# The lower half of every split weight tile on VectorE alone, in a fused gMLP, sparse-attention and differential-attention kernel

## The chip, the cores and the metric

The kernel runs on one core of one Trainium2 chip. The metric is the device time of one execution in microseconds (us), as the median over the runs shown; each run's time comes with a profile of one execution. The engines are TensorE (PE, with its weight loads as PEld), VectorE (DVE), ScalarE (ACT), GpSimd (POOL) and the DMA queue of SyncE (SP).

## What is computed

512 tokens of width 1024 pass through three layers, all in fp32:

```
first_block, layer 0:  x += g1 * rms(gmlp(mod(rms(x))));      x += g2 * rms(relu(h @ w1)^2 @ w2)
first_block, layer 1:  x += g1 * rms(nsa(mod(rms(x)), kv));   x += g2 * rms(relu(h @ w1)^2 @ w2)
second_block:          x += gate * (concat(stick_breaking(h), diff_attention(h)) @ w_out)
mod(h) = h * (1 + scale) + shift;  scale, shift, g = split(c_act @ ada_w + ada_b)
gmlp:  u, v = split(gelu(h @ w_in)); out = (u * (causal w_s @ layer_norm(v) + b_s)) @ w_out
nsa:   16 heads on 4 key/value groups; compressed, selected and windowed branches, gated
```

The weights are read once each: 205 MB over the execution by the profile's page.

## The kernel before

**Split products.** TensorE multiplies in fp32r, which holds fewer bits than fp32. So every operand of a large product is held as two tiles, an upper part `hi` (a copy of the source rounded to fp32r) and a lower part `lo = src - hi`, and one product is three matmuls: hi by hi, hi by lo, lo by hi. Three names of tiles recur: `wh`/`wl` are the two parts of a weight tile, `twh`/`twl` those of a weight tile in the tail of an output product, `ah`/`al` and `tah`/`tal` those of an activation that an output product reads. `raw` is the loaded weight before it is split; there are four places for it in the weight path (`RAW = 4`), and four each for `wh` and `wl` (`WT = 4`).

**Who makes the parts.** `splitw` (line 724) makes both from a source in SBUF. The upper part goes through `copyw`, which offers three engines (an ACT copy, a DVE copy, a POOL `tensor_scalar`). The lower part goes through `flex`, which offers two: a `tensor_sub` on DVE or on POOL. `splitw` is called for the weight tiles (`w_fm`, `w_rows`, `out_gemm`), the activations of the output products (`act_f32`), the normed activations (`h_split`, `gmlp`) and the probabilities of the attention stages (`ptl`, `ptc`, `sS`, with their upper parts `pth`, `ptc`, `sS`). Another function, `split` (line 719), for sources in PSUM, is fixed to ACT and DVE.

**What sets the order.** Nothing runs when it is written down: a recorder, `Rec`, keeps every operation with its readers and writers, and `Rec.order` lays all of them out with a list scheduler before the first instruction is issued. The scheduler has a modelled duration for each operation on each engine it may run on, adds 300 ns to an alternative on DVE and 100 ns to one on POOL when it compares alternatives, and knows that a two-input operation on POOL and one on DVE hold each other up. It runs twelve passes (`PASSES`), each with the due dates that the pass before gave, and keeps the pass with the earliest modelled end. So one operation that may no longer go to POOL can change the place of others on every engine, and also the order in which SP issues transfers. PE's order is fixed by hand within the attention stages (`KSEQ`, `NSEQ`, `SEQ`). Since the recorder issues all operations, each has the line L615 in the profile (activation tables L609), and rows are told apart by tile.

**The stages**, in time of the profile: set-up and the first layer's gMLP with its output product up to 190 us; the first feed-forward up to some 560; the key/value side of the sparse attention up to 640; the sparse attention (NSA) up to 880; the second feed-forward up to 1280; the second block's projections, stick-breaking and differential attention up to 1545; its output product to the end. At the start, `setup` builds eight `diag` tiles on DVE, from which PE makes `cb`, a broadcast of the conditioning vector; each weight row of `ada_w` is then multiplied with `cb` on DVE and summed (the operation `raw<-raw,cb`), which gives the vectors scale (`B`), shift (`S`) and gate (`G`). `wide` (line 948) spreads such a vector over all partitions for a stage's end: SP writes it to DRAM, then reads it back as two broadcasts (`S2w<-S` and then `S2w<-S2w`; likewise `B2w`, `G1w`). The gMLP's output product (`out_gemm` with `ATAIL = 8`) has all its eight weight rows as tail tiles, and chunk by chunk of 128 tokens passes through all eight; after each chunk the `boundary` makes the residual and the next layer's input `hx`, with `B2w` and `S2w`, which PE turns round (`tp`).

Of the kernel before, what the change touches and what calls it, by code (L numbers as in the profile page):

```python
# [26 lines left out]
F32 = mybir.dt.float32  # L27
# [643 lines left out]
class KB:  # L671
# [52 lines left out]
    def splitw(self, hi, lo, src):  # L724

        self.copyw(hi, src)
        self.flex("tensor_sub", lo, src, hi.bitcast(F32))

    def copyw(self, dst, src):

# [1345 lines left out]
```

## Time and profile before

| | before |
|---|---|
| median of 3 runs | 1586.44 us (1580.53 to 1587.76) |
| profiled execution: time, span of its instructions | 1586.38 us, 1584.6 us |
| granted clock of TensorE, mean over the span | 0.984 |
| busy share of the span | PE 95%, PEld 79%, DVE 70%, ACT 42%, POOL 27% |
| HBM traffic | 205 MB read, 6 MB written, 134 GB/s over the span |

The span is the time from the first to the last instruction; some 1.8 us of the execution lie around it. A group's mean duration can be read beside the shortest and the median of the same tile: where the mean lies far above, some of these instructions were held up while they ran. Which engine a wait is put down to is inferred from semaphore events.

### The profile page before, as it was taken

How to read it: one execution, taken by the hardware profiler on the slowest of the kernel's cores; microseconds unless marked ns; L12 is line 12 of the kernel's file. 1: busy time of each engine (PE TensorE's matmuls, PEld its weight loads, DVE VectorE, ACT ScalarE, POOL GpSimd, SP SyncE). 2: the span in 40 equal slices, each digit the busy share in tenths (PEclk: the TensorE clock that was granted, in tenths of full speed). 3: DMA queues.
4: the chain of work that ended last, by engine and by line, in shares of the span. 5: the costliest groups of instructions: out<-in, count | busy, mean ns of one | idle time of the engine just before them, and what ended most of it. 6: DMA issues, size and time to landing. Idle time of an engine off the chain costs nothing. (4 is left out here: it accounts for less than half of the span.)

```text
span 1584.6 us, 20197 instructions
## 1 busy us (share of the span) xinstructions
PE 1508.1 (95%) x7410; PEld 1256.2 (79%) x7410; DVE 1103.8 (70%) x1957; ACT 667.5 (42%) x1443; POOL 425.7 (27%) x415
## 2 busy tenths in 40 slices
PE   4997899999999999999998999999999999999988
PEld 3786788888888889787876898888888888878777
DVE  6897686567874478777886684555674568688882
ACT  4441342222121456577786332222111337667680
POOL 4044100000111131475676000000242024243560
PEclk9998899999999999999998999999999999999999
DMA  9756189537841071300115256538512251112312
GB/s 347 238 186 173 30 292 288 187 133 276 340 154 40 28 249 54 112 1 28 28 31 170 67 200 182 172 111 252 180 45 67 89 181 54 54 54 55 80 47 100
DMA packets 151395, 212.98 MB, mean 134 GB/s; under 512 B 49536, under 2 KB 110208, under 8 KB 151296
## 3 DMA queue, kind: packets, MB, share of 16 engines
q1 hardware_dynamic: 151296, 211.69, 41.7%
q8 instruction: 58, 0.95, 0.3%
q14 instruction: 41, 0.34, 0.1%
HBM read 205.33 MB, written 6.34 MB: 134 GB/s over the span
## 5 line engine op out<-in xcount | busy, mean ns | idle before, releaser
L615 DVE TENSOR_TENSOR wl<-raw,wh 128x1024 fp32r<-128x1024 f32 x176 | 230.9, 1315 | 55.7 <-PE fmps L615 18.5
L615 DVE CAST wh<-raw 128x1024 fp32r<-128x1024 f32 x118 | 88.7, 752 | 123.5 <-PE fmps L615 96.7
L615 PE MATMUL acc<-wh,ah 128*128 128x512 f32 x432 | 168.9, 392 | 0.0
L615 PE MATMUL acc<-wl,ah 128*128 128x512 f32 x432 | 168.6, 392 | 0.0
L615 DVE SCALAR_TENSOR_TENSOR raw<-raw,cb 128x1024 f32<-128x1024 f32 x112 | 146.4, 1329 | 6.7 <-DMA raw<-in_kv_ada_w_dram 6.0
L615 PE MATMUL acc<-wh,al 128*128 128x512 f32 x432 | 134.5, 391 | 0.0
L615 ACT ACTIVATE r<-fmps 128x512 f32<-128x512 f32 x64 | 38.4, 599 | 210.7 <-PE fmps L615 210.7
L615 POOL TENSOR_TENSOR al<-hid,ah 128x512 fp32r<-128x512 f32 x10 | 16.9, 1694 | 401.2 <-ACT ah L615 388.8
L615 PE MATMUL acc<-twh,tah 128*128 128x512 f32 x272 | 107.2, 402 | 3.3 <-DVE twh L615 3.3
L615 PE MATMUL acc<-twl,tah 128*128 128x512 f32 x272 | 107.3, 403 | 3.1 <-DVE twl L615 3.1
L615 PE MATMUL fmps<-hfh,wl 128*128 128x512 f32 (+1 forms) x288 | 106.0, 368 | 2.3 <-DVE wl L615 2.3
L615 PE MATMUL fmps<-hfl,wh 128*128 128x512 f32 (+1 forms) x288 | 105.6, 367 | 0.0
L615 PE MATMUL fmps<-hfh,wh 128*128 128x512 f32 (+1 forms) x288 | 105.4, 368 | 0.1
L615 PE MATMUL fmps<-hf1l,wh 128*128 128x512 f32 (+1 forms) x288 | 105.2, 366 | 0.0
L615 PE MATMUL fmps<-hf1h,wl 128*128 128x512 f32 (+1 forms) x288 | 105.2, 366 | 0.0
L615 PE MATMUL fmps<-hf1h,wh 128*128 128x512 f32 (+1 forms) x288 | 104.8, 365 | 0.0
L615 ACT CAST ah<-hid 128x512 fp32r<-128x512 f32 x47 | 29.1, 619 | 157.7 <-PE acc L615 157.7
L615 PEld LDWEIGHTS acc<-wl,ah 128*128 128x128 f32 x432 | 81.6, 189 | 16.9
L615 PEld LDWEIGHTS acc<-wh,ah 128*128 128x128 f32 x432 | 81.4, 189 | 16.8
L615 PEld LDWEIGHTS acc<-wh,al 128*128 128x128 f32 x432 | 81.4, 189 | 16.7
L615 PE MATMUL acc<-twh,tal 128*128 128x512 f32 x272 | 88.2, 400 | 3.2 <-DVE tal L615 3.2
L615 ACT CAST wh<-raw 128x1024 fp32r<-128x1024 f32 x57 | 59.3, 1049 | 55.9 <-PE fmps L615 25.7
(561 smaller groups left out, 3995.0 us busy)
## 6 DMA issues: line engine op xcount, KB each, us to landing
raw<-in_ada_w_dram SPq DMA_DIRECT2D x40, 1024.0 KB, 7.5
raw<-in_ff_w_in_dram SPq DMA_DIRECT2D x32, 1024.0 KB, 10.5
raw<-in_ff_w_out_dram SPq DMA_DIRECT2D x32, 1024.0 KB, 5.0
raw<-in_w_in_dram SPq DMA_DIRECT2D x16, 1024.0 KB, 5.6
raw<-in_w_ada_dram SPq DMA_DIRECT2D x12, 1024.0 KB, 11.1
raw<-in_a_w_in_dram SPq DMA_DIRECT2D x8, 1024.0 KB, 8.6
raw<-in_ada_w_dram SPq DMA_DIRECT2D x16, 512.0 KB, 11.9
raw<-in_kv_ada_w_dram SPq DMA_DIRECT2D x8, 1024.0 KB, 14.2
```

The source lines that it names most:

```text
L615: getattr(real[e], m)(*a, **k)
```

## The change

`splitw` makes the lower part on DVE always. Nothing else is edited; the order of everything is derived anew by the same rule.

```
@@ -724,7 +724,7 @@
     def splitw(self, hi, lo, src):
 
         self.copyw(hi, src)
-        self.flex("tensor_sub", lo, src, hi.bitcast(F32))
+        self.dve.tensor_sub(lo, src, hi.bitcast(F32))
```

In the order lists, 87 subtractions leave POOL: 30 of 128x1024 (`wl` 18, `twl` 12), 45 of 128x512 (`al` 11, `tal` 18, `hbl` 3, `hkl` 1, `vl` 3, `dV` 3, `ptl` 6) and 12 smaller (`sS` 3, `ptc` 8, one of a compression weight). DVE's list has all of them. POOL has 22 more one-input copies and scalings than before, ACT 21 fewer; PE has the same 7408 matmuls and transposes, with local changes of order. Six of the 128x1024 and nine of the smaller subtractions that leave POOL lie in the NSA stage, eleven and seventeen in the second block.

First place: DVE at the start, from the `diag` tiles on (`hx` is the scaled input, `x_87` and `x_94` two chunks of it, `cbp` the PSUM of `cb`). Before:

```order
L615 TENSOR_SCALAR diag<-ident,cc 128x128 x8
L615 SCALAR_TENSOR_TENSOR xrs<-rt,xrs 128x4
L615 TENSOR_SCALAR hx<-x_87,xrs 128x512
L615 COPY cb<-cbp 128x512
L615 SCALAR_TENSOR_TENSOR raw_100,S_186<-raw_100,cb 128x1024
L615 SCALAR_TENSOR_TENSOR raw_100,B_215<-raw_100,cb 128x1024
```

and now:

```order
L615 TENSOR_SCALAR diag<-ident,cc 128x128 x8
L615 SCALAR_TENSOR_TENSOR xrs<-rt,xrs 128x4
L615 TENSOR_SCALAR hx<-x_87,xrs 128x512
L615 TENSOR_SCALAR hx<-x_94,xrs 128x512
L615 TENSOR_TENSOR wl<-raw,wh 128x1024 x2
L615 SCALAR_TENSOR_TENSOR raw_100,B_192<-raw_100,cb 128x1024
L615 SCALAR_TENSOR_TENSOR raw_100,S_207<-raw_100,cb 128x1024
```

The first two `wl` stand on DVE between `diag` and the first dot product; before, they were POOL's, whose list there was `wh`, `wl` twice, `hx`, and is now `wh` and four `hx`. The copy of `cb` that DVE had went to ACT.

Second place: SP ahead of and during the gMLP's output product (the weight of that product is `a_w_out`; `G_546` and `G_520`, `B_834` and `B_876`, `S_1000` and `S_981` are the same vectors before and now). A piece of the difference:

```order
+L615 DMA raw<-in_a_w_out_dram 128x2x1024
+L615 DMA G1w<-G_520 128x8x1
+L615 DMA B2w<-B_876 128x8x1
 L615 DMA raw<-in_a_w_out_dram 128x2x1024
 L615 DMA G1w<-G1w 128x512 x2
-L615 DMA raw<-in_a_w_out_dram 128x2x1024 x3
-L615 DMA S2w<-S_1000 128x8x1
+L615 DMA B2w<-B2w 128x512 x2
+L615 DMA raw<-in_a_w_out_dram 128x2x1024 x2
+L615 DMA S2w<-S_981 128x8x1
 L615 DMA S2w<-S2w 128x512 x2
-L615 DMA B2w<-B_834 128x8x1
-L615 DMA B2w<-B2w 128x512 x2
```

The first `a_w_out` is ahead of the write of `G1w` (before, behind it), `B2w` is written and read back ahead of the last weights, and `S2w` alone is left for the end, where `S2w` and then `B2w` stood.

Third place: DVE through the gMLP's output product (`mx` and `sg` belong to the mixing ahead of it). Before:

```order
L615 CAST twh<-raw 128x1024
L615 SCALAR_TENSOR_TENSOR mx<-pm,lngb,E 128x512 x2
L615 TENSOR_TENSOR twl<-raw,twh 128x1024
L615 SCALAR_TENSOR_TENSOR mx<-pm,lngb,E 128x512
L615 TENSOR_TENSOR sg_722<-sg_722,mx 128x512
L615 TENSOR_TENSOR twl<-raw,twh 128x1024
L615 SCALAR_TENSOR_TENSOR raw,S_1000<-raw,cb 128x1024
L615 TENSOR_TENSOR tal<-sg_722,tah 128x512
L615 SCALAR_TENSOR_TENSOR raw,S_1000<-raw,cb 128x1024
L615 TENSOR_TENSOR twl<-raw,twh 128x1024
L615 TENSOR_TENSOR S_1000<-S_1000,vcol 128x8
```

and now:

```order
L615 TENSOR_TENSOR twl<-raw,twh 128x1024
L615 TENSOR_TENSOR tal<-sg_730,tah 128x512
L615 TENSOR_TENSOR twl<-raw,twh 128x1024
L615 TENSOR_TENSOR tal<-sg_937,tah 128x512
L615 TENSOR_TENSOR twl<-raw,twh 128x1024
L615 SCALAR_TENSOR_TENSOR raw,S_981<-raw,cb 128x1024
L615 TENSOR_TENSOR tal<-sg_937,tah 128x512 x2
L615 TENSOR_TENSOR S_981<-S_981,vcol 128x8
L615 CAST twh<-raw 128x1024
L615 TENSOR_TENSOR twl<-raw,twh 128x1024 x2
```

All eight `twl` and eight `tal` of this product are DVE's (six and four before), its `B` is done ahead of the product, and the sum that ends `S` stands behind six of the eight `twl` where it stood behind three.

## Rows read from the trace of the kernel before

**Rows 1.** Page, part 1: busy time, share of the span, instructions of each engine.

```profile
PE 1508.1 (95%) x7410; PEld 1256.2 (79%) x7410; DVE 1103.8 (70%) x1957; ACT 667.5 (42%) x1443; POOL 425.7 (27%) x415
```

**Rows 2.** Stretches: length; PE, PEld, DVE, ACT, POOL busy us; clock, DMA share, GB/s.

```profile
0.00:45.00 45.00, 21.47 (x83) 15.88 (x84) 28.85 (x52) 21.46 (x35) 17.33 (x14) 0.95 0.94 327
45.00:80.00 35.00, 35.00 (x152) 28.82 (x151) 28.91 (x58) 16.03 (x28) 2.78 (x2) 0.97 0.73 241
...
125.00:190.00 65.00, 50.41 (x239) 41.27 (x238) 46.90 (x63) 18.25 (x36) 26.66 (x14) 0.84 0.41 100
...
800.00:880.00 80.00, 72.19 (x392) 56.90 (x391) 57.95 (x157) 52.76 (x140) 49.69 (x59) 0.94 0.36 100
880.00:1280.00 400.00, 399.80 (x1885) 335.22 (x1883) 241.50 (x344) 102.12 (x198) 44.01 (x24) 1.00 0.45 143
...
1480.00:1545.00 65.00, 58.41 (x314) 49.15 (x313) 55.61 (x109) 47.85 (x126) 43.33 (x30) 0.97 0.14 49
```

**Rows 3.** A group by shape: count, busy us, mean ns; idle time before, and its releasers.

```profile
L615 DVE TENSOR_TENSOR wl<-raw,wh 128x1024 fp32r<-128x1024 f32 x176 | 230.9, 1315 | 55.7 <-PE fmps L615 18.5 <-ACT wh L615 18.5 <-PE acc L615 11.5
```

**Rows 4.** Tiles on DVE: shortest, median and longest duration in ns.

```profile
L615 DVE TENSOR_TENSOR wl<-raw,wh x176: 1194/1225/3415, 46.3 to 1542.9; 128x1024 fp32r<-128x1024 f32 x176
...
L615 DVE TENSOR_TENSOR al<-hid,ah x38: 671/684/1773, 333.6 to 1193.3; 128x512 fp32r<-128x512 f32 x38
...
L615 DVE TENSOR_SCALAR diag<-ident,cc x8: 273/275/2380, 13.0 to 18.6; 128x128 f32<-128x128 f32 x8
```

**Rows 5.** What PE waited for: us in total, times, longest.

```profile
PE tp L615 <- DVE hx L615: 5.2, 2, 5.0
...
PE acc L615 <- DVE tal L615: 3.2, 1, 3.2
PE acc L615 <- DVE twl L615: 3.1, 2, 1.9
```

**Rows 6.** Timeline of the start: start, us, engine, operation [idle before].

```profile
12.99 5.85 DVE L615 TENSOR_SCALAR diag<-ident,cc 128x128 f32<-128x128 f32 x8
13.14 4.64 POOL L615 TENSOR_TENSOR wl<-raw,wh 128x1024 fp32r<-128x1024 f32 x2
...
24.36 3.37 DVE L615 SCALAR_TENSOR_TENSOR raw<-raw,cb 128x1024 f32<-128x1024 f32 x1
...
29.73 1.12 PE L615 MATMUL vps<-wh,hh 128*128 128x512 f32 x2 [2.59 <-ACT hh L615]
```

**Rows 7.** Timeline of the gMLP's output product and boundary, SP and DVE.

```profile
156.70 1.21 DVE L615 SCALAR_TENSOR_TENSOR raw<-raw,cb 128x1024 f32<-128x1024 f32 x1
...
156.80 0.37 SPq L615 DMA_DIRECT2D S2w<-S  x1
167.92 1.23 SPq L615 DMA_DIRECT2D S2w<-S2w  x2
...
178.14 0.80 SPq L615 DMA_DIRECT2D B2w<-B2w  x2
...
182.07 0.69 DVE L615 TENSOR_TENSOR hx<-x,B2w 128x512 f32<-128x512 f32 x1 [5.54 <-DMA B2w<-B2w]
```

**Rows 8.** Timeline of the differential attention.

```profile
1500.64 2.57 POOL L615 TENSOR_TENSOR twl<-raw,twh 128x1024 fp32r<-128x1024 f32 x1
...
1500.88 2.88 DVE L615 SCALAR_TENSOR_TENSOR dPA<-dPA,rr 128x512 f32<-128x512 f32 x1
...
1522.70 0.74 DVE L615 SCALAR_TENSOR_TENSOR dPA<-dPA,rr 128x512 f32<-128x512 f32 x1
```

**Rows 9.** Chain that ended last: start, us, engine, tile.

```profile
1540.91 1.36 POOL al L615
...
1544.89 35.20 PE acc L615 x155
```

**Rows 10.** Timeline of the stick-breaking attention, POOL's copies beside DVE.

```profile
1315.60 1.64 DVE L615 TENSOR_TENSOR wl<-raw,wh 128x1024 fp32r<-128x1024 f32 x1
...
1316.58 0.94 POOL L615 TENSOR_SCALAR ptc<-saC 128x256 fp32r<-128x256 f32 x1 [0.40 <-POOL sbh L615]
```

More of the change, by code (lines that the diff above doesn't have):

```diff
@@ L726, in splitw @@
         self.copyw(hi, src)
-        self.flex("tensor_sub", lo, src, hi.bitcast(F32))
+        self.dve.tensor_sub(lo, src, hi.bitcast(F32))
     def copyw(self, dst, src):
```

## Prediction

> **What bounds the kernel now.** I read the page's busy times first. PE is busy 1508.1 of 1584.6 us and DVE 1103.8 [rows 1], so a faster DVE pays only where PE stands still, 76.5 us in all. The stretches tell where [rows 2]. In the second feed-forward (880 to 1280 us) PE is busy 399.8 of 400 us: whatever DVE does there, nothing is to be had. From 45 to 80 us it is busy 35 of 35. It stands still 23.5 us in the first 45 us, 14.6 us between 125 and 190 (the gMLP's output product), 7.8 us between 800 and 880 (end of NSA) and 6.6 us between 1480 and 1545 (differential attention). Between 125 and 190 the granted clock is also 0.84: since the levels are 1.2 and 2.4 GHz, 32% of that stretch, 20.8 us, ran at the lower one, in which half of the work, 10.4 us, is lost.
>
> The rows of single operations then tell what POOL's subtractions cost. A `wl` on DVE takes 1.225 us in the median, 1.315 in the mean and 3.415 at the longest [rows 3, 4]; 176 times the difference of mean and median is 16 us of being held up on this tile alone. Neighbours show it better. Eight `diag` take 5.85 us while POOL makes two `wl` in 4.64 us [rows 6]; the median `diag` is 0.275 us [rows 4]. One `dPA` takes 2.88 us beside a `twl` on POOL, another 0.74 us [rows 8]. So a subtraction that spares DVE 1.2 us can hold it up by about 2 us, and it takes POOL itself some 2.3 to 2.6 us [rows 6, 8].
>
> **What the change moves.** By the order lists 30 subtractions of 128x1024 and 57 smaller ones go to DVE. At 1.225 us and at most 0.684 us (the `al` [rows 4], of 128x512) that is 36.8 + 39.0 = at most 75.8 us more work on DVE. Against it stands the hold-up that goes away. No single row has its sum, so the bounds are nil and all the time those 87 took on POOL, at some 2.4 us for a wide one and half of that for the others 140 us. I take it to be about as large as the added work, because the rows on neighbours show 3.65 us for two subtractions at the start and 2.1 us for one later, against 1.225 each. DVE's busy time should therefore stay near 1100 us, and what counts is the place. By stage:
>
> *Start, -4 us (0 to -6).* PE's first matmul waits for `diag`. Eight of them undisturbed take 8 x 0.275 = 2.2 us, so 3.65 us go. The dot product at 24.36 us took 3.37 us [rows 6], undisturbed 1.21 [rows 7]: 2.16 us go. The two `wl` (2.45 us) and one more `hx` (at most 0.68) now lie on DVE ahead of the dot products. They fit into the time in which DVE waits for `cb` to come from PE; if they do not, 3.1 us of the 5.8 are given back. I take 4. The start of the `vps` products at 29.73 us [rows 6] moves up by that, and as PE is busy without a gap from 45 us on, the gain is kept if the loads keep up: DMA is 94% busy in the first 45 us, 73% after [rows 2], which is why the lower bound is nil.
>
> *gMLP's output product, -10 us (0 to -22).* PE waits there 3.2 us for `tal`, 3.1 for `twl`, and 5.0 for `hx` [rows 5]. The first two are waits for DVE while POOL holds it up; I expect these 6.3 us to go. The third is a wait of `hx` for `B2w`, whose read back was issued at 178.14 us, behind `S2w`, and which set `hx` free at 182.07 [rows 7]. Now `B2w` goes out before, and `S2w` alone is late. From its write to its read 11.1 us passed, the two reads took 1.23 us to issue, and from the end of `B2w`'s issue at 178.94 to `hx` another 3.1 us. If `S` is ready at about the same time as before, 156.8 us, `S2w` is there at 156.8 + 11.1 + 1.2 + 3.1 = 172.2, ten us ahead of what `hx` waited for. `S` now stands behind three more `twl` (3.7 us) and four more `tal` (2.7 us), so it has 6.4 us less, and the margin stays positive: the 5.0 us go as well. With 6.3 that is 11.3 us. The write of two vectors now stands on SP ahead of the second weight load, so a late `B` would hold up weights; this I set at 1.3 us against it, about one `twl`. So 10. The clock may give up to 10.4 us more if PE no longer stands still there; together with all 14.6 us of idle time it is 25, and I stop the bound at 22 because the `hx` chain of the boundary stays.
>
> *Feed-forwards, 0 us.* DVE is busy 241.5 of 400 us in the second [rows 2], and its part of the 75.8 us hides beside PE. If that cover failed, it would show as PE idle in a stretch which now has none.
>
> *NSA, +2 us (-3 to +8).* Six wide and nine smaller subtractions, at most 13.5 us, go to DVE, whose chain from scores to `ptl` is what PE waits for. PE has 7.8 us of idle time at its end and a clock of 0.94 [rows 2]. POOL's copies of probabilities are small, so here less hold-up goes away than work comes.
>
> *Second block, -3 us (-6.6 to +6).* Eleven wide and seventeen smaller ones, at most 25.1 us, come. But the chain that ends last runs through held-up operations such as the `dPA` above (2.14 us over its own time). The ceiling of the last stretch is its idle time, 6.6 us; I take about half.
>
> *End, -0.7 us (0 to -0.7).* The last `al` before the output product is on POOL, 1.36 us, and on the chain [rows 9]; on DVE it is 0.684.
>
> The sum is -4 - 10 + 2 - 3 - 0.7 = -15.7 us. Against the profiled execution, 1586.38 us (span 1584.6 and 1.8 around it), that gives 1570.7, and I say **1571 us**. The median shown, 1586.44, is the same within 0.1.
>
> **A rule that speaks against it.** A `wl` on DVE took 1.64 us beside a one-input copy on POOL of 0.94 us [rows 10]: 0.4 us over the median. So POOL's copies hold DVE up too, though less than its subtractions, and POOL has 22 more of them. The Trainium skill, "SBUF — State Buffer", section "Who interferes with whom", says that a DVE instruction with two SBUF inputs contends with any GpSimd instruction that reads SBUF, the first to issue keeping the shared ports to its end. By that rule each subtraction moved to DVE would become one more that POOL's copies can block, and the sum would come out near no change; the row at 1315.60 us agrees that a copy blocks, but with a quarter of what the `dPA` row shows for a subtraction.
>
> **Rivals.** *No relief (1584 us).* POOL's copies take the place of its subtractions, and DVE is held up as before. Each of the 87 subtractions, and its neighbours, may meet a copy at 0.4 us, 87 x 0.4 = 35 us of hold-up, which with 75.8 us of work outweighs a relief at its lower end. Then only what the order itself gives is left, `B2w` ahead of the product (5 us), less what NSA loses (2 to 3). For it: the row above. Against it: at the start POOL now runs only copies of half the width.
>
> *DVE becomes the bound in the attention stages (1596 us).* 13.5 + 25.1 = 38.6 us come onto DVE where PE waits for it in turns. The start and the gMLP still give 14. If 24 of the 38.6 us come through to PE, the time is 1586.4 - 14 + 24 = 1596. It decides at 14 us coming through, 36%: above that, the kernel is slower. For it: DVE is already busy 58 of 80 and 56 of 65 us at the two ends [rows 2]. Against it: the removed hold-up lies in the same stretches.
>
> *Everything goes (1553 us).* The gMLP stage gives 22, the start 5, the second block 6: 1586.4 - 33 = 1553. For it: a PE that does not stand still keeps its clock. Against it: waits that end are as a rule followed by the next one.
>
> **How the numbers follow.** The forecast's own case gets 0.54, no relief 0.22, the attention bound 0.14, everything 0.10. What a measurement of this kernel can tell from no change is about 0.5%, 8 us: faster is below 1578.5, slower above 1594.3. Of the forecast's case nearly all, 0.51, is faster, and all of the fourth: 0.61. Slower is most of the third and a little of the first two: 0.14. The rest, 0.25, is the same. The range goes from 1554, which cuts half of the fourth case, to 1590, which cuts most of the third: with the tails of the others some 0.2 is left out.
>
> **What would show it.** Right: no `TENSOR_TENSOR` of `wl`, `twl`, `al`, `tal` on POOL; median and mean of `wl` on DVE within 30 ns; the eight `diag` in about 2.2 us and `vps` starting near 26; PE's waits for `tal` and `twl` in the gMLP and for `hx` gone or below 2 us; DVE's busy time 1080 to 1130 us. Wrong: DVE busy above 1150 (no relief); PE waiting more than 14 us longer for `ptl`, `ptc` or `wl` in the attention stages (the slower rival); a new wait of weights behind `B2w`'s write near 125 us, or of `hx` for `S2w`.

## The result, and the profile after

The changed kernel takes **1545.21 us** (median of 4 runs, 1544.52 to 1546.29), the kernel before 1585.66 us (4 runs, 1580.53 to 1587.76): a ratio of 0.975, 95% interval 0.9726 to 0.9775. That is 40 us, where 15.7 were forecast, and 8.8 us below the lower end of the range. The profiled execution has a span of 1544.5 us.

The page of the changed kernel, busy times, answers to [rows 1]:

```profile
PE 1496.9 (97%) x7410; PEld 1248.8 (81%) x7410; DVE 1088.8 (70%) x2038; ACT 657.2 (43%) x1422; POOL 294.0 (19%) x355
```

DVE has 81 more instructions and is busy 15 us *less*; POOL is relieved of 132 us. PE does the same work in 11.2 us less (at a higher clock) and stands still 47.6 us instead of 76.5, 28.9 less: the two make the 40.1 us of the span. The same stretches of time as in [rows 2], the columns as there; since the changed kernel runs ahead, by up to 33 us at 880 us, a stretch holds in part other work than before:

```profile
0.00:45.00 45.00, 28.99 (x126) 22.61 (x127) 34.01 (x77) 26.21 (x40) 10.08 (x12) 1.00 0.93 328
45.00:80.00 35.00, 33.96 (x151) 27.81 (x149) 30.20 (x81) 19.88 (x44) 5.85 (x5) 1.00 0.82 263
...
125.00:190.00 65.00, 60.40 (x316) 49.57 (x315) 57.57 (x96) 26.89 (x60) 14.48 (x9) 1.00 0.53 170
...
800.00:880.00 80.00, 74.64 (x346) 60.45 (x346) 55.52 (x119) 35.63 (x90) 22.24 (x27) 0.89 0.43 127
880.00:1280.00 400.00, 400.00 (x1884) 335.31 (x1883) 227.83 (x342) 102.97 (x189) 14.50 (x16) 1.00 0.45 145
```

The clock, 0.95 and 0.84 in the first and third of these stretches before, is now 1.00, and PE stands still less in both (16.0 and 4.6 us, where it was 23.5 and 14.6). Between 800 and 880 us it is 0.89, lower than before; over the whole NSA stage it is 0.97 where it was 0.98. The tiles of [rows 3, 4], by shape and by duration:

```profile
L615 DVE TENSOR_TENSOR wl<-raw,wh 128x1024 fp32r<-128x1024 f32 x194 | 240.4, 1242 | 41.3 <-PE fmps L615 18.5 <-ACT wh L615 14.8 <-POOL wh L615 0.8
```

```profile
L615 DVE TENSOR_TENSOR wl<-raw,wh x194: 1195/1225/2119, 16.2 to 1495.9; 128x1024 fp32r<-128x1024 f32 x194
```

The mean of a `wl` lies 17 ns over the median, where it lay 90. The start, which answers to [rows 6]:

```profile
13.19 1.65 DVE L615 TENSOR_SCALAR diag<-ident,cc 128x128 f32<-128x128 f32 x8
14.11 3.78 PE L615 MATMUL cbp<-diag,shared 128*128 128x512 f32 x4 [14.11 <-DVE diag L615]
...
15.01 7.18 POOL L615 TENSOR_SCALAR hx<-x,xrs 128x512 f32<-128x512 f32 x4 [1.95 <-DVE xrs L615]
...
16.19 2.75 DVE L615 TENSOR_TENSOR wl<-raw,wh 128x1024 fp32r<-128x1024 f32 x2
...
18.87 1.21 DVE L615 SCALAR_TENSOR_TENSOR raw<-raw,cb 128x1024 f32<-128x1024 f32 x1
```

The eight `diag` take 1.65 us instead of 5.85, so that PE's first product starts 4.0 us earlier (14.11 us, where it was 18.11), and the two `wl` fill the time until `cb` is there.

PE's waits, which answer to [rows 5] (total, times, longest):

```profile
PE acc L615 <- DVE tal L615: 1.1, 2, 0.6
...
PE tp L615 <- DVE hx L615: 1.1, 1, 1.1
...
PE acc L615 <- DVE twl L615: 0.5, 1, 0.5
```

All three, 11.5 us together before, are nearly gone. To place the gain, the span is cut at eight landmarks on PE, the first or last start of a matmul in the trace. Lengths in us:

| stage, up to | before | after | difference | forecast |
|---|---|---|---|---|
| first `vps` | 29.7 | 23.6 | -6.1 | -4 |
| first `acc` of the gMLP's output product | 109.7 | 104.1 | -5.6 | (in the line above) |
| first product of the feed-forward (`fmps<-hfh`) | 65.7 | 50.9 | -14.8 | -10 |
| first NSA scores (`sC<-K,Q`) | 455.5 | 451.3 | -4.2 | 0 |
| second feed-forward (`fmps<-hf1h`) | 254.1 | 252.1 | -2.1 | +2 |
| last of the second block's `tmc` | 536.6 | 537.2 | +0.6 | -3, with the line below |
| last of the differential attention (`dpo`) | 80.3 | 71.4 | -8.9 | |
| last `acc` | 48.1 | 49.1 | +1.0 | -0.7 |

### The profile page after: what moved, and what is told of

It reads as the page before. It is cut to its first block, busy times and chain, and to the rows that moved or that the text cites. A ratio compares the mean times of both kernels' runs of the same rounds, so it can differ in the third digit from the quotient of the medians.

```text
span 1544.5 us, 20161 instructions
## 1 busy us (share of the span) xinstructions
PE 1496.9 (97%) x7410; PEld 1248.8 (81%) x7410; DVE 1088.8 (70%) x2038; ACT 657.2 (43%) x1422; POOL 294.0 (19%) x355
## 4 chain that ended last, share of the span: by engine, by line
PE 76%; DVE 8%; ACT 3%; issue 2%; POOL 1%; DMA 0%; POOLq 0%; DVEq 0%; ACTq 0%
PE acc L615 30%; PE fmps L615 25%; PE qps L615 4%; PE tmc L615 4%; PE po L615 2%; PE sgps L615 2%; DVE wl L615 2%; DVE ptl L615 2%; PE vps L615 1%; PE tmb L615 1%; PE kps L615 1%; PE sB L615 1%; PE tp L615 1%; PE sA L615 1%; PE tA L615 1%
## 5 line engine op out<-in xcount | busy, mean ns | idle before, releaser
L615 DVE TENSOR_TENSOR wl<-raw,wh 128x1024 fp32r<-128x1024 f32 x194 | 240.4, 1242 | 41.3 <-PE fmps L615 18.5
L615 PE MATMUL acc<-wh,ah 128*128 128x512 f32 x432 | 168.9, 391 | 0.0
L615 PE MATMUL acc<-wl,ah 128*128 128x512 f32 x432 | 168.6, 390 | 0.0
L615 DVE CAST wh<-raw 128x1024 fp32r<-128x1024 f32 x118 | 82.9, 703 | 119.9 <-PE fmps L615 93.7
L615 DVE SCALAR_TENSOR_TENSOR raw<-raw,cb 128x1024 f32<-128x1024 f32 x112 | 137.1, 1248 | 11.7 <-DMA raw<-in_kv_ada_w_dram 7.9
L615 PE MATMUL acc<-wh,al 128*128 128x512 f32 x432 | 133.8, 390 | 0.0
L615 ACT ACTIVATE r<-fmps 128x512 f32<-128x512 f32 x64 | 38.2, 597 | 206.9 <-PE fmps L615 206.9
L615 PE MATMUL fmps<-hfh,wl 128*128 128x512 f32 (+1 forms) x288 | 105.5, 366 | 1.1 <-DVE wl L615 1.1
L615 PE MATMUL acc<-twh,tah 128*128 128x512 f32 x272 | 105.1, 392 | 1.1 <-ACT tah L615 1.1
L615 PE MATMUL acc<-twl,tah 128*128 128x512 f32 x272 | 105.4, 393 | 0.6 <-DVE twl L615 0.5
L615 PE MATMUL fmps<-hfl,wh 128*128 128x512 f32 (+1 forms) x288 | 105.2, 366 | 0.2 <-DVE hfl L615 0.2
L615 PE MATMUL fmps<-hf1l,wh 128*128 128x512 f32 (+1 forms) x288 | 105.2, 366 | 0.0
L615 PE MATMUL fmps<-hf1h,wl 128*128 128x512 f32 (+1 forms) x288 | 105.2, 366 | 0.0
L615 PE MATMUL fmps<-hfh,wh 128*128 128x512 f32 (+1 forms) x288 | 105.0, 366 | 0.0
L615 PE MATMUL fmps<-hf1h,wh 128*128 128x512 f32 (+1 forms) x288 | 104.8, 365 | 0.0
L615 ACT CAST ah<-hid 128x512 fp32r<-128x512 f32 x48 | 29.7, 619 | 159.4 <-PE acc L615 159.4
L615 PEld LDWEIGHTS acc<-wh,ah 128*128 128x128 f32 x432 | 81.5, 189 | 16.9
L615 POOL TENSOR_SCALAR tah<-hid 128x512 fp32r<-128x512 f32 x5 | 5.5, 1112 | 470.4 <-DMA raw<-in_ff_w_out_dram 206.5
L615 PEld LDWEIGHTS acc<-wl,ah 128*128 128x128 f32 x432 | 81.4, 188 | 16.8
L615 PEld LDWEIGHTS acc<-wh,al 128*128 128x128 f32 x432 | 81.3, 188 | 16.7
L615 PE MATMUL acc<-twh,tal 128*128 128x512 f32 x272 | 86.8, 394 | 1.1 <-DVE tal L615 1.1
L615 ACT CAST wh<-raw 128x1024 fp32r<-128x1024 f32 x57 | 59.8, 1050 | 55.3 <-PE fmps L615 32.0
```

The source lines that it names most:

```text
L615: getattr(real[e], m)(*a, **k)
```

## The experiments

**Engine and order apart.** Two kernels split the change. In the first, order and engines are those of the kernel before; only the 87 subtractions are given to DVE when they are issued. In the second, the order is that of the changed kernel, and the same 87 go to POOL (`o.low` marks a lower part, and `LOW` is the list of the 87 numbers).

```
     rec.order()
+    for o in rec.ops:
+        if o.low and o.eng[0] == "pool":      # first kernel
+            o.eng = o.alts[0]
...
+        if o.seq in LOW:                      # second kernel
+            o.eng = ("pool",) + o.eng[1:]
```

> The order and every other engine choice of the kernel before; only the 87 subtractions that POOL made are issued on DVE, each at its old place in the order. Hold-up theory (what counts is that POOL no longer holds DVE up): most of the gain of 40 us comes without any new order, 1550 to 1562 us, and TensorE's clock stays up to 650 us. Order theory (what counts is the order derived anew, with B2w's write and the first a_w_out load moved up): 1575 to 1590 us, since B2w still waits behind S2w.

> The order of the changed kernel, but the 87 subtractions that POOL made before are issued on POOL again, each at its new place. Hold-up theory: DVE is held up again, 1578 to 1600 us. Order theory: the gain stays, 1548 to 1560 us.

Measured: the first 1576.79 us (ratio 0.9945, 0.9928 to 0.9961), the second 1575.92 us (0.9941, 0.9927 to 0.9956). The first lies where the order theory put it, the second where neither did, so neither holds. The engine alone gives 8.0 us, the order alone 8.9, both 40: 23 us come only from the two together. The first kernel's page, and its waits of PE (its lines count one more, L616 for L615):

```profile
PE 1510.5 (96%) x7410; PEld 1256.2 (80%) x7410; DVE 1090.1 (69%) x2044; ACT 667.4 (42%) x1443; POOL 261.2 (17%) x328
```

```profile
PE tp L616 <- DVE hx L616: 5.0, 1, 5.0
...
PE acc L616 <- DVE twl L616: 2.7, 2, 2.4
PE acc L616 <- DVE tal L616: 2.5, 1, 2.5
```

With 87 more subtractions, at most 75.8 us of work, DVE is busy 13.7 us less than in [rows 1]: by these two figures up to 89 us of its busy time before were hold-up. And yet the time falls by 8 us only: the waits of [rows 5] stay, `hx` 5.0 (5.0 before), `tal` 2.5 (3.2), `twl` 2.7 (3.1), and the NSA stage takes longer (table below). The second kernel shows the reverse. Its waits now name POOL:

```profile
PE acc L615 <- POOL tal L615: 5.5, 2, 5.2
PE dot L615 <- DVE gate L615: 4.1, 1, 4.1
PE tp L615 <- POOL hx L615: 4.0, 2, 3.8
```

By stage, with the landmarks of the table above, the three kernels differ from the kernel before by (us):

| stage, up to | subtractions on DVE alone | order alone | both |
|---|---|---|---|
| first `acc` of the gMLP's output product | -7.3 | -7.5 | -11.7 |
| first product of the feed-forward | -0.7 | -6.9 | -14.8 |
| first NSA scores | -1.9 | -2.5 | -4.2 |
| second feed-forward | +7.2 | +2.0 | -2.1 |
| last of the second block's `tmc` | -0.6 | +3.4 | +0.6 |
| last of the differential attention | -5.3 | -3.5 | -8.9 |
| last `acc` | -0.6 | +6.2 | +1.0 |

At the start the two overlap by 3.1 us. What neither gives alone, some 22 us in the profiled executions, lies in NSA (11.3 us), in the gMLP's output product (7.2), in the last output product (4.6) and ahead of the last `tmc` (2.3). In NSA each half by itself costs time, and that of the first kernel is hardly a wait. The stage in the kernel before and in the first kernel, columns as in [rows 2]:

```profile
660.60:914.70 254.10, 242.13 (x1317) 196.94 (x1316) 190.37 (x517) 169.09 (x452) 140.57 (x192) 0.98 0.21 59
650.70:912.00 261.30, 248.07 (x1318) 200.79 (x1317) 198.11 (x531) 169.68 (x452) 118.89 (x178) 0.95 0.21 58
```

PE stands still 1.3 us longer and is busy 5.9 us longer, at a granted clock of 0.95 where it was 0.98. Why the clock was lower there is not shown.

**By stage.** A flag in `splitw` makes lower parts on DVE alone in the gMLP and leaves the choice after it, or the reverse (the edit against the kernel before).

```
-        self.flex("tensor_sub", lo, src, hi.bitcast(F32))
+        if self.only:
+            self.dve.tensor_sub(lo, src, hi.bitcast(F32))
+        else:
+            self.flex("tensor_sub", lo, src, hi.bitcast(F32))
...
         self.gmlp(rows, hf)
+        self.only = False      # True in the complement
```

> Lower parts on DVE alone in the gMLP (set-up to the first boundary), on either engine after it, order derived anew. By the landmarks of the two traces the first feed-forward starts 26.5 us earlier in the changed kernel: if the stages add up, 1585.7 - 27 = 1559 us (1555 to 1563). If the gain hangs on the whole order, anything outside that.

> The complement: either engine in the gMLP, DVE alone after it, order derived anew. If the stages add up, the gain is the remaining 13 us: 1572 us (1568 to 1577). If the gain hangs on the whole order, anything outside that.

Measured: 1568.9 us (0.9896, 0.9881 to 0.9911) and 1559.56 us (0.9837, 0.9822 to 0.9851). Both miss. The gains add up to 41 us, yet not by stage: the first is 13.8 us ahead at the first `acc` of the gMLP's output product, but gains nothing in that product, which took 66.7 us (before 65.7), since PE stood still for a weight:

```profile
155.29 1.22 PE L615 MATMUL acc<-twh,tah 128*128 128x512 f32 x2 [12.14 <-DVE twh L615]
```

SP shows why. The columns are start, duration, operation:

```profile
130.96 0.37 SPq L615 DMA_DIRECT2D B2w<-B  x1
141.64 0.81 SPq L615 DMA_DIRECT2D B2w<-B2w  x2
142.56 0.38 SPq L615 DMA_DIRECT2D raw<-in_a_w_out_dram  x1
143.04 0.41 SPq L615 DMA_DIRECT2D G1w<-G  x1
155.31 0.81 SPq L615 DMA_DIRECT2D G1w<-G1w  x2
```

A read-back waits until its write has landed, 10.7 and 12.3 us here, and whatever stands behind it on SP waits too: the last weight load does. The complement starts as late as before (first `vps` at 29.8 us), yet its output product takes 59.3 us, 6.4 less, with the choice left open there and six of that product's subtractions on POOL, as many as before: by the order alone. It has the differential attention at 71.4 us, as short as in the changed kernel.

**Was it one lucky order?** One number of the planner is moved by 10 ns either way, in both kernels.

```
-    "act": dict(pe=375, act=132, dve=131, pool=160, sp=150),
+    "act": dict(pe=385, act=132, dve=131, pool=160, sp=150),      # and 365
```

> The kernel before, with one number of the planner moved a little (the modelled lag from ACT to PE 385 instead of 375 ns), which shuffles the order and changes nothing else. If the order before was just an unlucky one: well below 1585, down to 1565 us. If every order with subtractions on POOL suffers: 1578 to 1598 us.

> The changed kernel with the same small move of the planner's number (385). If the 40 us were one lucky order: 1556 to 1575 us. If the absence of POOL's subtractions makes every order good: 1541 to 1552 us.

> The kernel before with the number moved the other way (365 ns). Unlucky order: down to 1565 us. Hold-up in every order: 1578 to 1598 us.

> The changed kernel with the number moved the other way (365 ns). Lucky order: 1556 to 1575 us. Every order good: 1541 to 1552 us.

Measured, against a kernel before of 1585.93: with 385, 1579.32 (0.9954, 0.9936 to 0.9972) and 1544.14 (0.974, 0.9724 to 0.9757); with 365, 1573.7 (0.9938, 0.9917 to 0.996) and 1539.51 (0.9707, 0.9693 to 0.9722). The change gives 35 and 34 us within the pairs. So some 5 to 6 us of the 40 are luck of the first order, and 34 to 35 come in the shifted orders too: three orders out of three with the subtractions on DVE lie within 1539 to 1546 us. The stages of the three pairs (us):

| stage, up to | before | before, 385 | before, 365 | changed | changed, 385 | changed, 365 |
|---|---|---|---|---|---|---|
| first `acc` of the gMLP's output product | 139.4 | 140.4 | 140.2 | 127.7 | 127.5 | 127.7 |
| first product of the feed-forward | 65.7 | 63.1 | 57.6 | 50.9 | 50.8 | 50.3 |
| first NSA scores | 455.5 | 452.3 | 453.8 | 451.3 | 452.2 | 451.0 |
| second feed-forward | 254.1 | 253.0 | 250.7 | 252.1 | 250.3 | 247.7 |
| last of the second block's `tmc` | 536.6 | 541.3 | 540.8 | 537.2 | 535.2 | 535.2 |
| last of the differential attention | 80.3 | 74.8 | 74.8 | 71.4 | 71.4 | 71.4 |
| last `acc` | 48.1 | 48.0 | 48.7 | 49.1 | 49.1 | 49.1 |

The start gains about 12 us in every pair. In the differential attention only 3.4 of the 8.9 us come in every pair; the other 5.5 are the luck of a poor order before. The gMLP's output product gains 14.8, 12.2 and 7.3 us, but the three changed orders are alike on SP there (G and B written side by side near 114 us, S alone near 146). The order of the gMLP experiment, also with all lower parts of that stage on DVE, had another one and gained nothing, so this part of the gain needs the order too. The order with 385 and subtractions on POOL has `B2w` ahead of `S2w`, and its product still takes 63.1 us; the one with 365 has it behind, and takes 57.6 without a wait for `hx`: the place of `B2w` by itself does not give the gain.

**B2w back behind S2w.** The changed kernel with three transfers moved at issue.

```
     rec.order()
+    late = [o for o in rec.ops if o.seq in (874, 875, 876)]        # B2w: write, two reads
+    rest = [o for o in rec.ops if o.seq not in (874, 875, 876)]
+    at = next(i for i, o in enumerate(rest) if o.seq == 881) + 1   # last read of S2w
+    rec.ops = rest[:at] + late + rest[at:]
```

> The changed kernel and its order, with the write of B2w and its two reads moved back behind those of S2w, as in the kernel before. The prediction put 5.0 us on this place. If hx waits for B2w again: 1549 to 1554 us, with PE waiting 4 us or more for hx in the first boundary. If DVE has hx late anyway: within 2 us of 1545.

Measured: 1560.65 us (0.9842, 0.9826 to 0.9858), 15.4 us more than the changed kernel, three times what the prediction had put on this place. SP, DVE and PE:

```profile
146.37 0.37 SPq L615 DMA_DIRECT2D S2w<-S  x1
157.41 0.81 SPq L615 DMA_DIRECT2D S2w<-S2w  x2
158.28 0.42 SPq L615 DMA_DIRECT2D B2w<-B  x1
169.10 0.80 SPq L615 DMA_DIRECT2D B2w<-B2w  x2
```

```profile
172.71 1.44 DVE L615 TENSOR_TENSOR hx<-x,B2w 128x512 f32<-128x512 f32 x2 [15.98 <-DMA B2w<-B2w]
```

```profile
176.30 1.09 PE L615 MATMUL tp<-ident,hx 128*128 128x128 f32 x4 [15.06 <-DVE hx L615]
```

In the changed kernel G and B are written together and share one wait, and S follows alone:

```profile
113.78 0.37 SPq L615 DMA_DIRECT2D G1w<-G  x1
114.20 0.57 SPq L615 DMA_DIRECT2D B2w<-B  x1
114.82 1.73 SPq L615 DMA_DIRECT2D raw<-in_a_w_out_dram  x1
124.34 0.81 SPq L615 DMA_DIRECT2D G1w<-G1w  x2
...
146.96 0.37 SPq L615 DMA_DIRECT2D S2w<-S  x1
157.38 0.82 SPq L615 DMA_DIRECT2D S2w<-S2w  x2
```

Two chains run through this stage: the product, whose splits DVE makes, and the vectors, which SP spreads. It ends with the later one. Before, both were late: taking POOL's subtractions away alone left 65.0 us (the kernel with the old order), `B2w` late with everything else new 67.4, the new order with POOL's subtractions 58.8, both 50.9.

**The rest of POOL's two-input operations.** In the changed kernel, `flex` offers POOL only for `tensor_scalar`.

```
-        self.R.add([("dve", m, a, k), ("pool", m, a, k)])
+        self.R.add([("dve", m, a, k)] + ([("pool", m, a, k)] if m == "tensor_scalar" else []))
```

> The changed kernel, in which the remaining two-input operations that could run on either engine (hx times B2w, sg times mx, the saB and saC sums, dqkr, mix times gate) are DVE's too; order derived anew. If any two-input operation on POOL costs more than it spares: 1538 to 1544 us. If the rest are placed well and DVE is late: 1546 to 1556 us.

Measured: 1543.27 us (0.9734, 0.9717 to 0.975). The interval overlaps that of the changed kernel, 0.9726 to 0.9775: no difference is shown. Together with the planner's 365:

> Both steps that were faster than the changed kernel together: no two-input alternative on POOL, and the planner's lag of 365 ns. If their gains add: 1545.2 - 2 - 5.7 = 1537.5 us. If both are shuffles of the order: anywhere from 1537 to 1548 us.

Measured: 1542.41 us (0.9734, 0.9718 to 0.975), above the 1539.51 of the 365 alone. The gains do not add; both are shuffles of the order.

**POOL's copies (e9).** In the changed kernel, `copyw` loses its POOL alternative.

```
-        self.R.add([("act", "copy", (dst, src), {}), ("dve", "tensor_copy", (dst, src), {}),
-                    ("pool", "tensor_scalar", (dst, src, 1.0, 1.0), dict(op0=OP.mult, op1=OP.mult))])
+        self.R.add([("act", "copy", (dst, src), {}), ("dve", "tensor_copy", (dst, src), {})])
```

> The changed kernel, in which upper parts are copied on ACT or DVE only, never on POOL; order derived anew. If POOL's copies hold DVE up about as its subtractions did: DVE's busy time falls although it has more copies, 1530 to 1542 us. If the copies cost little and spare DVE and ACT work: 1546 to 1565 us.

Measured: 1548.31 us (0.9767, 0.9753 to 0.9782). DVE is busy 1085.0 us, 3.8 less, though it has 33 more instructions, twelve of them copies of 128x1024 at 0.7 us. So the copies had held it up by some 12 us or more (an estimate, 3.8 + 12 x 0.7), little beside the subtractions, and a `wl` is hardly shorter:

```profile
L615 DVE TENSOR_TENSOR wl<-raw,wh 128x1024 fp32r<-128x1024 f32 x194 | 238.6, 1233 | 43.7 <-PE fmps L615 21.0 <-ACT wh L615 16.6
```

The time as such tells nothing of copies, for the order has the fault of the gMLP experiment again: a weight load behind the read-back of `B2w`, PE waiting 12.8 us. The gMLP's output product takes 66.4 us, 15.4 more than in the changed kernel; everything else together takes 11.4 us less, most of it in NSA (246.2 us, where the changed kernel has 252.1) and from there to the last `tmc` (529.9, where it has 537.2). Whether that is the copies' hold-up or the order was not taken apart.

```profile
PE acc L615 <- DVE twh L615: 12.8, 1, 12.8
```

**SP's order put right by hand (e13, e14).** In e9, the load goes ahead of `B2w`'s write; and in a second one the three writes also come ahead of the three read-backs. (`to(o)` is the tile that a transfer writes, `read` is `B2w`'s first read-back, `free` the place of the last use of the load's buffer before it; the last three lines are the second kernel's alone, and put `move` behind the write of `S2w`.)

```
     rec.order()
+    load = next(o for o in dma[dma.index(read):] if o.alts[0][2][0].buf.name == "raw")
...
+    at = rec.ops.index(load)
...
+    rec.ops.insert(min(free + 1, at), rec.ops.pop(at))
...
+    move = [o for n in ("B2w", "G1w") for o in dma if to(o).name == n and not to(o).dram]
+    rec.ops = [o for o in rec.ops if o not in move]
...
+    rec.ops[at:at] = move
```

> The kernel e9 (no copies on POOL) and its order, with one transfer moved on SP: the last a_w_out load goes ahead of the write of B2w. In e9 PE waited 12.8 us for that load's upper part. If the load sets the stage: 1548.3 - 12 = 1536 us (1534 to 1539). If the pairs of write and read-back set it (S2w was usable at 176.2 us, its write held behind the read-back of G1w): only some 3 us, 1543 to 1547, with PE or DVE waiting for G1w or S2w instead.

> The kernel e13, with the read-backs of B2w and G1w moved behind the write of S2w, so that the three writes are followed by the three read-backs and SP waits once instead of three times. If the pairs set the stage: 10 to 15 us below e9, 1533 to 1538. If the load alone did: the same as e13. If neither: 1548.

Measured: 1546.44 us (0.9753, 0.9737 to 0.9769) and 1545.01 us (0.9742, 0.9728 to 0.9757). The load was not the bound: once it comes early, PE waits 11.3 us for `hx` instead, in the first kernel because G and S follow as two more pairs:

```profile
145.22 0.37 SPq L615 DMA_DIRECT2D G1w<-G  x1
156.29 0.80 SPq L615 DMA_DIRECT2D G1w<-G1w  x2
157.18 0.38 SPq L615 DMA_DIRECT2D S2w<-S  x1
167.85 0.80 SPq L615 DMA_DIRECT2D S2w<-S2w  x2
```

```profile
PE tp L615 <- DVE hx L615: 11.3, 1, 11.3
```

The second is 3.3 us below the kernel without POOL's copies where 10 to 15 were expected. `S2w` no longer binds, but `G1w` does: G is ready on DVE at 143 us only, and its copy is usable 20 us later.

```profile
143.12 0.37 SPq L615 DMA_DIRECT2D G1w<-G  x1
...
154.26 0.79 SPq L615 DMA_DIRECT2D G1w<-G1w  x2
```

```profile
162.73 0.69 DVE L615 TENSOR_TENSOR z<-acc,G1w 128x512 f32<-128x512 f32 x1 [16.09 <-DMA G1w<-G1w]
```

So it is the pairs of write and read-back that set this stage, and what counts is when DVE has a vector's sums ready as much as the order on SP. In the changed kernel G is written at 113.8 us, 14 us ahead of the product.

The fastest version is the changed kernel with the planner's lag at 365 ns, 1539.51 us (0.9707, 0.9693 to 0.9722). It is a better order found by a small shift, not a better rule.

## Why the prediction was wrong

The direction and most of the signs that it named hold: the eight `diag` in about 2.2 us (1.65), `vps` near 26 (23.6), `wl` within 30 ns of its median (17), waits for `tal`, `twl` and `hx` below 2 us (1.1, 0.5 and 1.1), DVE busy 1080 to 1130 us (1088.8). The relief of DVE was sized right: about as large as the added work, by the kernel with the old order up to 89 against 76 us.

**The step that failed is the sum, "-4 - 10 + 2 - 3 - 0.7": it counts time in which PE stands still, too little of it, and puts the clock at nothing.** PE stood still 28.9 us less, and its busy time fell by 11.2 us because the granted clock rose. The prediction had the clock only in a bound of one stage and among the rivals, as a reason for the fast one. The largest mis-sized term is the start, -4 with a lower bound of -6, which measured -11.7. By terms, from the table of stages, the forecast is short by 7.7 us at the start, 4.8 in the gMLP's output product, 4.2 in the key/value side and ahead of it, 4.1 in NSA, and 3.6 in the second block with its end:

- *Start, -4 (0 to -6):* 11.7 us up to the first `acc`. The mechanism is right, the held-up `diag` and dot products: in the old order with the subtractions on DVE the eight `diag` take 1.66 us, the dot products 1.2, and `vps` comes 4.8 us earlier. Mis-sized: of the 5.8 us of hold-up the term gave 1.8 back for `wl` and `hx`, which were hidden, and `vps` came 6.1 us earlier. The other 5.6 us lie between there and the first `acc`, where the term had nothing: PE stands still 2.9 us less and is busy 2.7 us less, at a granted clock of 1.00 where it was 0.97. The bound by DMA did not bind (share 0.93 and 0.82).
- *gMLP's output product, -10 (0 to -22):* 14.8 us, within its bounds, of which 8.5 are PE's idle time and 6.3 its busy time at a clock of 1.00 where it was 0.85. The sum of waits was thus near, the clock left out, and the working fails in two places. The waits for `tal` and `twl` do not end with POOL's subtractions: without any and in the old order they are 2.5 and 2.7 us still. There POOL's other operations still hold DVE up, and a dot product for `S` stands among the splits (lines below). And the 5.0 us on `hx` were the price of `B2w`'s place in a stage in which the product was late as well. With an early product the same place costs 15.4 us.
- *Feed-forwards, 0 us:* right for both. The key/value side behind the first one gained 3.5 us (27.2 us ahead at its start, 30.7 at the first NSA scores); the prediction had no term there.
- *NSA, +2 (-3 to +8):* -2.1 us, the other sign. In the old order the stage took 261.3 us against 254.1, but not because DVE was late: PE's waits hardly grow, its clock is lower.
- *Second block, -3 (-6.6 to +6):* -8.3 us without its end, -7.3 with it. The ceiling was PE's idle time in the last stretch alone. In the differential attention PE stands still 6.2 us less, near that ceiling, and is busy 2.7 us less at a clock of 1.00 where it was 0.98.
- *End, -0.7:* the last output product took 1.0 us more.

The gMLP's output product before and after, columns as in [rows 2]:

```profile
139.40:205.10 65.70, 54.42 (x216) 42.92 (x217) 53.46 (x77) 22.91 (x51) 22.89 (x11) 0.85 0.32 89
127.70:178.60 50.90, 48.14 (x218) 37.94 (x218) 43.66 (x74) 21.13 (x47) 11.39 (x7) 1.00 0.40 121
```

DVE and POOL in it, in the kernel with the old order and the subtractions on DVE (with POOL idle, a `twl` takes 1.2 us there):

```profile
136.83 2.30 DVE L616 TENSOR_TENSOR twl<-raw,twh 128x1024 fp32r<-128x1024 f32 x1
139.05 2.05 DVE L616 SCALAR_TENSOR_TENSOR raw<-raw,cb 128x1024 f32<-128x1024 f32 x1
```

```profile
136.33 1.72 POOL L616 TENSOR_TENSOR sg<-sg,mx 128x512 f32<-128x512 f32 x1
138.02 2.01 POOL L616 TENSOR_SCALAR twh<-raw 128x1024 fp32r<-128x1024 f32 x1
```

Adding the terms is a second fault. In the gMLP's output product, which ends with the later of two chains, 7.2 of the 14.8 us come from neither half of the change alone; a list of single waits does not tell this. That the two one-sided kernels give 8.0 and 8.9 us, 17 together and close to the 15.7 forecast, is chance: by stage they give 14.8 at the start where 4 were forecast, and lose 9.2 in NSA and 5.6 at the end.

Of the rivals, *no relief* fell: DVE's busy time went down. (The copy's 0.4 us, by which that rival was priced, is a fifth of the 2.14 us in the `dPA` row, not a quarter.) *DVE becomes the bound* fell as well: from 640 to 1545 us PE waited 5.9 us for `ptl` from DVE in the kernel before, 6.6 in the old order with the subtractions on DVE, and 2.6 in the changed kernel. *Everything goes* (1553) came nearest, and in part for the reason it gave: 11.2 of the 40.1 us are a clock that stays up. It was still 8 us too slow. The page "SBUF — State Buffer" of the Trainium skill, section "Who interferes with whom", has POOL's one-input copies contend as well. The runs agree that there is such hold-up and show it small: with all copies of upper parts off POOL, `wl` goes from a mean of 1242 to 1233 ns, against 1315 with the subtractions there.

What stays open: why each half of the change costs time in NSA and both together do not, why the granted clock is lower there in the old order, and what a kernel would take whose SP order is derived with the price of a read-back in mind; none was run.

## What to carry to other kernels

Where two chains end a stage together, ask of every wait what the time would be if all the others were gone; the sum of single waits can be far from the gain of a change that relieves several. Price PE's clock as a term of its own wherever it is below 1.00. A slower engine that takes work off a busier one can cost it as much as it takes (here up to 89 us against 76), and such hold-up is found by comparing mean and median of the same tile on the busier engine. A write that is read back on the same queue held up all that stood behind the read-back, for 8.9 to 12.3 us here: put such writes side by side, early, with the loads ahead of the read-backs.

## What the runs showed of the hardware

- The 87 two-input subtractions on POOL cost DVE up to 89 us of 1104 in this kernel, up to about 1 us for each; and DVE holds POOL up in turn: four `hx` beside two `wl` took 7.18 us on POOL, 1.8 each, where one took 0.98 us in the kernel before.
- A small vector's write and read-back through DRAM takes 8.9 to 12.3 us from the issue of the write to that of the read, where nothing stands between them, and 14 to 20 us from the write to the first use.
